# Where GpSimd applies the gains and biases of two inner norms, and which engine splits one weight piece

## The chip, the core and the metric

The kernel runs on one core of one Trainium2 chip. The metric is device time in microseconds (us): the median of 3 runs of the kernel before is 1522.11 us (1521.24 to 1522.42). A core has TensorE (PE in the profile, its weight loads PEld), VectorE (DVE), ScalarE (ACT), GpSimd (POOL) and SyncE (SP), which here only issues DMAs.

## What is computed

The reference is a two-layer decoder trunk on 256 tokens of width 1024. Layer 0 mixes tokens with a state-space layer and a GLU, then runs a dense SwiGLU. Layer 1 mixes with a three-group dilated attention and runs a top-2-of-8 expert SwiGLU. After each of these four sublayers comes the same residual and norm:

```
h = _s5_mixer(x, ...)
x = _layer_norm(DEEPNORM_ALPHA * x + h, ln_g[0, 0], ln_b[0, 0])     # norm 0
f = _swiglu(x, ...)
x = _layer_norm(DEEPNORM_ALPHA * x + f, ln_g[0, 1], ln_b[0, 1])     # norm 1
h = _dilated_attention(x, ...)
x = _layer_norm(DEEPNORM_ALPHA * x + h, ln_g[1, 0], ln_b[1, 0])     # norm 2
f = _moe(x, ...)
x = _layer_norm(DEEPNORM_ALPHA * x + f, ln_g[1, 1], ln_b[1, 1])     # norm 3
```

with `_layer_norm` = (x - mean) / sqrt(var + eps) * g + b. The change concerns norms 0 and 1, called the first and the second norm here.

## The kernel before, in words

**Tokens and norms.** The residual lies in SBUF as two tiles `x1[0]`, `x1[1]` of 128 tokens x 1024 (the program names them `xx`). At a norm, for each tile t: `residual_steps` (L749, L750) adds the sublayer's output and takes statistics on VectorE; `ln_power` (L755 to L757) finishes the statistics, and GpSimd takes one power (128x1, tile `lr_`); `ln_root` (L763 to L765) corrects it on VectorE; `ln_scale` (L772) subtracts the mean and multiplies by the root, in two halves of 512 columns. Then `flips` (L782) lets TensorE transpose the eight 128x128 blocks, and `turned` (L792 to L798) applies gain and bias on the transposed side: blocks 0 to 3 by ScalarE (L792), 4 to 7 by VectorE (L793), then ScalarE rounds to fp32r (L797) and VectorE takes the remainder (L798), so that `xT[0]` and `xT[1]` hold high and low part. The next matmuls read these. Their order over blocks is `korder` = 0, 4, 1, 5, ...

The residual itself stays without gain and bias until `ln_affine` (L775, L776) puts them on, since the next norm adds to it: on GpSimd, a multiplication and an addition of 128x1024 for each tile, with the gain and bias rows from the tile `gb` (both rows on every partition, 1 MB, loaded by GpSimd's queue).

**First norm.** For t = 0 and then 1 the loop at L871 to L885 does `flips`, `turned` and 48 matmuls into `ab` (the first two weight pieces of the SwiGLU, L885). While t = 0 is turned, VectorE interleaves what is left of the residual of t = 1 (`weave`). At t = 1, after `turned`, `ws.split` splits the next weight pieces. Behind the loop GpSimd's queue holds, in this order: `ln_affine` of both tiles, the load of the second norm's rows into `gb` (L890), and the bias tables of the attention: 64 DMAs `skew<-vecs` (L897) and 32 DMAs `raw<-skew` (L903, L907).

**Second norm.** The loop at L971 and after does the same with 24 matmuls into `pv` (values, L970) for each tile. After `turned` of t = 0 one weight piece is split with GpSimd as the subtracting engine; behind the loop stands `ln_affine` of both tiles, and then the pool of `gb` is closed; three raw tiles (`ring4`) are laid where it was.

**Weights.** `Stream` loads pieces of 1 MB (`raw` tiles) on SyncE's queue in a fixed order, `seq`, into whichever tile is free, oldest first. `split` turns a piece into a pair of fp32r tiles (L109 a copy on ScalarE, L110 a subtraction, on VectorE unless another engine is given). `get` gives back what the last call used, splits as far ahead as there are pairs, and hands out the next piece. Every matmul on split operands is done as three passes.

**Attention.** A loop over 8 head pairs `hp`: three query-key pieces (L1100, one for each dilation group, in the order 1, 2, 0 but 0, 1, 2 at hp = 0), then two value pieces (L970), with the steps of the pair before (scores, softmax, transposes, products with the values) interleaved. GpSimd does two copies a pair (L1016). Behind the attention come norm 2, the routing and the experts, whose weight pieces (`in_moe`) come through the same stream.

Of the kernel before, what the change touches and what calls it, by code (L numbers as in the profile page):

```python
# [20 lines left out]
D, S, G, P, C, H = 1024, 256, 64, 64, 16, 16  # L21
# [19 lines left out]
def gorder(hp):  # L41

    return (1, 2, 0) if hp else (0, 1, 2)
# [107 lines left out]
def trunk(ctx: ExitStack, tc: tile.TileContext, a, out, dbg=None):  # L151
    nc = tc.nc
    ctx.enter_context(tc.manual_schedule())
    V, A, T, Q = nc.vector, nc.scalar, nc.tensor, nc.gpsimd

    def dump(name, ap):
        if dbg and name in dbg:
            nc.gpsimd.dma_start(out=dbg[name], in_=ap)

    def pool(name, bufs=1, **k):  # L160
        return tc.tile_pool(name=name, bufs=bufs, reuse_waits="tile", **k)
# [9 lines left out]
    seq = []  # L171
# [4 lines left out]
    for i in range(3 * NFP):  # L176
        seq.append((a["ffn"][i], 2048, True))
    for hp in range(8):
        qk = [(a["qk"][3 * hp + g], 2048, True) for g in gorder(hp)]
        v = [(a["wv"][2 * hp + i], 1536, True) for i in range(2)]  # L180
        seq += v + qk if hp == 0 else qk + v
# [3 lines left out]
    def gain_bias(i):  # L185

        return bass.AP(a["ln"].tensor, i * 2 * D, [[0, 128], [1, 2 * D]])
# [39 lines left out]
    ws = Stream(nc, seq + moe_seq, raw, pairs)  # L227
# [27 lines left out]
    M_, A_, S_ = ALU.mult, ALU.add, ALU.subtract  # L255
# [419 lines left out]
    def passes(hl_s, hl_m):  # L675
        return ((hl_s[0], hl_m[0]), (hl_s[0], hl_m[1]), (hl_s[1], hl_m[0]))
# [42 lines left out]
    x1 = [xx[:, D * i:D * i + D] for i in range(2)]  # L719
# [5 lines left out]
    gb = gbs.enter_context(pool("gb", side="right")).tile([128, 2 * D], F32, name="gb")  # L725
# [21 lines left out]
    def residual_steps(t, n, src):  # L747
        xs = x1[t][:, n * 512:n * 512 + 512]
        return [lambda: V.scalar_tensor_tensor(out=xs, in0=xs, scalar=ALPHA, in1=src, op0=M_, op1=A_),  # L749
                lambda: V.bn_stats(out=lst[:, t, n, :], in_=xs)]  # L750
# [21 lines left out]
            V.tensor_scalar(out=xs, in0=xs, scalar1=lmv[:, t, 0:1], scalar2=lr_[:, t, 1:2], op0=S_, op1=M_)  # L772

    def ln_affine(t, eng, gb=gb):
        eng.tensor_tensor(out=x1[t], in0=x1[t], in1=gb[:, 0:D], op=M_)  # L775
        eng.tensor_tensor(out=x1[t], in0=x1[t], in1=gb[:, D:2 * D], op=A_)  # L776

    def flips(t, pp):

        tr = [pp.tile([128, 4, 128], F32, tag="tr", name="tr") for _ in range(2)]  # L780
        for k in range(8):
            T.transpose(tr[k // 4][:, k % 4, :], x1[t][:, k * 128:k * 128 + 128], ident)  # L782
        return tr

    def turned(i, t, tr, lnw=None, plain=None):

        cs = slice(t * 128, t * 128 + 128)
        f_ = lnw.tile([128, 8, 128], F32, tag="lnf", name="lnf") if plain is None else plain[:, :, cs]
        for j in range(5):
            if j < 4:  # L790
                g_, b_ = ([lnT[:, i, q, k:k + 1] for k in (j, 4 + j)] for q in range(2))
                A.activation(out=f_[:, j, :], in_=tr[0][:, j, :], func=ACTF.Identity, scale=g_[0], bias=b_[0])  # L792
                V.tensor_scalar(out=f_[:, 4 + j, :], in0=tr[1][:, j, :], scalar1=g_[1], scalar2=b_[1], op0=M_, op1=A_)  # L793
                yield
            if plain is None and j:
                ks = slice(j - 1, j + 4, 4)
                A.copy(out=xT[0][:, ks, cs], in_=f_[:, ks, :])  # L797
                V.tensor_tensor(out=xT[1][:, ks, cs], in0=f_[:, ks, :], in1=xT[0][:, ks, cs], op=S_)  # L798
                yield

    def weave(main, other):
        for _ in main:
            if other:
                (other.pop(0) or int)()
        for f in filter(None, other):
            f()

    def after(r):
        return [None, None, r[0], None, r[1], None, lambda: ln_power(1), lambda: ln_scale(1)]
# [48 lines left out]
    def gated_in(ab):  # L858
        sl = fw.tile([128, 2, 256], F32, tag="sl", name="sl")
        A.activation(out=sl, in_=ab[0], func=ACTF.Silu)  # L860
        V.tensor_tensor(out=sl, in0=sl, in1=ab[1], op=M_)
        return sl
# [21 lines left out]
                for ip, (s_, m_) in enumerate(passes([q[:, k, cs] for q in xT], [q[:, k, :] for q in w13[i]])):  # L884
                    T.matmul(ab[i][:, t, :], lhsT=s_, rhs=m_, start=(k == 0 and ip == 0), stop=(k == 7 and ip == 2))  # L885
    lns.close()
    for t in range(2):
        ln_affine(t, Q)
        dump(f"x1_{t}", x1[t])
    Q.dma_start(out=gb, in_=gain_bias(1))  # L890
    h0 = gated_in(ab)


# [4 lines left out]
    for i, b in enumerate(btab):  # L898
        hs = slice(4 * i, 4 * i + 4)
        for cl in range(2):  # L900
            pp = slice(64 * cl, 64 * cl + 64)
            for c0, b0, nb in ((0, 0, 4), (384, 4, 2)):
                Q.dma_start(out=b[pp, :, c0:c0 + 64 * nb],  # L903
                            in_=skew[:, hs, b0 + 1 - cl:b0 + nb + 1 - cl, :].rearrange("t h b s -> t h (b s)"))
            for g in range(2):
                c0 = 256 + 64 * (g ^ cl)
                Q.dma_start(out=b[pp, :, c0:c0 + 64], in_=skew[:, hs, 7 + g, :])  # L907

    accs = ExitStack()
    def down_proj(t, n, w, j):  # L910
# [6 lines left out]
    for fp in range(1, NFP):  # L917
        ab = []
        for i in range(2):
            w = [q.rearrange("p (k c) -> p k c", c=256) for q in ws.get()]  # L920
# [18 lines left out]
        if fp < NFP - 1:  # L939
            w = [q.rearrange("p (f c) -> p f c", c=1024) for q in ws.get()]  # L940
# [24 lines left out]
    w = [[q[:, 0:1536].rearrange("p (k c) -> p k c", c=384) for q in ws.get(1 - hf, hold=hf == 1)] for hf in range(2)]  # L965

    def values(t, kk, w):
        x_ = [q[:, kk, t * 128:t * 128 + 128] for q in xT]
        for ip, (s_, m_) in enumerate(passes(x_, [q[:, kk % 4, :] for q in w])):
            T.matmul(ov[t], lhsT=s_, rhs=m_, start=(kk == 0 and ip == 0), stop=(kk == 7 and ip == 2))  # L970

    for t in range(2):
        weave(turned(1, t, flips(t, ptn), lnw),
              [] if t else after(residual_steps(1, 1, acc[1][1])))
        ws.split(ws.cur + 9 * t, V if t else Q)
        for kk in korder:
            values(t, kk, w[kk // 4])
    trs.close()
    accs.close()
    for t in range(2):  # L980
        ln_affine(t, Q)
    for t in range(2):
        dump(f"x2_{t}", x1[t])
    gbs.close()
    xps.close()
    ring4 = ctx.enter_context(pool("ring4", side="right"))
# [6 lines left out]
    with ExitStack() as e:  # L993
# [96 lines left out]
        prev = iter(())  # L1090
        for hp in range(8):
            par = hp % 2
            for g in gorder(hp):
                w = [q.rearrange("p (k c) -> p k c", c=256) for q in ws.get()]
                o = pqk.tile([128, 2, 256], F32, tag="qk", name="qkp")
                for qk in range(2):
                    for k in range(8):
                        w_ = [q[:, k, qk * 128:qk * 128 + 128] for q in w]
                        for ip, (s_, m_) in enumerate(passes(w_, [q[:, k, :] for q in xT])):
                            T.matmul(o[:, qk, :], lhsT=s_, rhs=m_, start=(k == 0 and ip == 0), stop=(k == 7 and ip == 2))  # L1100
                        if k % 2 == 1:
                            next(prev, None)
                if g == 0:
                    undilated(o)
                else:
                    A.mul(out=qT[par][g], in_=o[:, 0, :], mul=0.125)
                    V.tensor_copy(out=kT[par][g], in_=o[:, 1, :])
            if hp:
                ov = [pv.tile([128, 512], F32, tag=f"v{t}", name=f"pv{t}")[:, 0:384] for t in range(2)]
                for hf in range(2):  # L1110
                    w = [q[:, 0:1536].rearrange("p (k c) -> p k c", c=384) for q in ws.get()]
                    for k in range(4):
                        for t in range(2):
                            values(t, 4 * hf + k, w)
                        next(prev, None)
            for _ in prev:
                pass
            if hp in (2, 4, 6):
                ws.add(bts[hp // 2 - 1:hp // 2])

            for t, f in ((0, A.copy), (1, V.tensor_copy)):
                v, lo_, hi_ = vt[par][t], slice(0, 64), slice(64, 128)
                f(out=v[lo_, 0:256], in_=ov[t][lo_, 0:256])
                f(out=v[hi_].rearrange("p (a b) -> p a b", b=128)[:, 0:3:2, :],
                  in_=ov[t][hi_, 0:256].rearrange("p (a b) -> p a b", b=128))
                f(out=v[hi_, 128:256], in_=ov[t][lo_, 256:384])
                f(out=v[lo_, 256:384], in_=ov[t][hi_, 256:384])
            prev = attn_steps(hp)
# [8 lines left out]
        for n in range(2):  # L1137
            w = [q.rearrange("p (k c) -> p k c", c=512) for q in ws.get()]
# [4 lines left out]
        w = [[q.rearrange("p (k c) -> p k c", c=512) for q in ws.get(9, hold=n == 1)] for n in range(2)]  # L1143
# [438 lines left out]
    with ExitStack() as e:  # L1582
# [11 lines left out]
        c = CAPS[E - 1]  # L1594
# [128 lines left out]
```

## Time and profile before

| what | value |
|---|---|
| median of 3 runs | 1522.11 us |
| the profiled execution's own time | 1521.36 us |
| its span, first to last instruction | 1519.6 us |
| busy: PE, PEld, DVE, ACT, POOL | 1435.5, 1043.3, 545.2, 384.4, 117.3 us |
| mean granted clock of TensorE | 0.978 of 2.4 GHz |

The profile's times count from the span's start. A busy PE is not a PE at its peak, since the ends of matmuls are modelled. The granted clock has two levels: 1.00 is 2.4 GHz, 0.50 is 1.2 GHz; a stretch with a mean between the two was partly at either.

### The profile page before, as it was taken

What the parts mean: (1) busy time and instruction counts of PE and PEld (TensorE: products, weight loads), DVE (VectorE), ACT (ScalarE), POOL (GpSimd) and SP (SyncE); (2) the same over time, 40 slices, a digit from 0 to 9 for tenths busy, and PEclk for the clock granted to TensorE, in tenths of its full rate; (3) what the DMA queues carried; (4) which work ended last, traced back from release to release, by engine and by line L of the source; (5) the groups of instructions that cost most, each with busy time, mean ns of one, the idle gap of its engine ahead of it and who ended that gap; (6) DMA issues with size and microseconds to landing.
All of it is one profiled execution on the core that took longest, in us unless ns stands there. A gap on an engine that the chain in (4) does not pass through costs nothing. (4 is left out here: it accounts for less than half of the span.)

```text
span 1519.6 us, 32295 instructions
## 1 busy us (share of the span) xinstructions
PE 1435.5 (94%) x14108; PEld 1043.3 (69%) x14108; DVE 545.2 (36%) x1021; ACT 384.4 (25%) x633; POOL 117.3 (8%) x156
## 2 busy tenths in 40 slices
PE   7769899998999999999999899999999999999996
PEld 6658799996999999865454466654566666666552
DVE  9998754447656666560020010010100100100103
ACT  6525444433555545420110000010100100100100
POOL 0110574004000000001000000000000000000001
PEclk9989899999999999989999999999999999999998
DMA  6008389553544454559999999999999999999995
GB/s 257 7 30 304 117 289 268 195 179 139 194 152 156 155 180 179 188 205 371 426 426 426 425 425 425 425 426 426 425 425 425 418 397 403 371 366 389 409 426 214
DMA packets 68412, 458.31 MB, mean 302 GB/s; under 512 B 9041, under 2 KB 9716, under 8 KB 15780
## 3 DMA queue, kind: packets, MB, share of 16 engines
q1 hardware_dynamic: 62752, 443.63, 72.7%
q0 software_dynamic: 4272, 9.92, 2.2%
q10 hardware_dynamic: 1236, 2.58, 0.5%
q8 instruction: 115, 1.88, 0.5%
q14 instruction: 37, 0.30, 0.1%
HBM read 454.97 MB, written 3.48 MB: 302 GB/s over the span
## 5 line engine op out<-in xcount | busy, mean ns | idle before, releaser
L1381 PE MATMUL a<-raw,xe 128*64 128x256 f32 (+1 forms) x7152 | 516.3, 328 | 9.0 <-DMA raw<-in_moe 8.3
L1381 PEld LDWEIGHTS a<-raw,xe 128*64 128x64 f32 (+1 forms) x7152 | 351.6, 124 | 163.4 <-issue 25.6
L1381 PE MATMUL y<-raw,h 128*32 128x256 f32 (+1 forms) x1792 | 255.7, 488 | 6.4 <-DMA raw<-in_moe 5.4
L1450 DVE TENSOR_TENSOR sl<-sl,a 128x256 f32<-128x256 f32 (+1 forms) x56 | 27.3, 488 | 564.8 <-PE a L1381 564.5
L110 DVE TENSOR_TENSOR sp<-raw,sp 128x2048 fp32r<-128x2048 f32 (+1 forms) x83 | 181.7, 2195 | 98.3 <-ACT sp L109 98.3
L1381 PEld LDWEIGHTS y<-raw,h 128*32 128x32 f32 (+1 forms) x1792 | 89.9, 123 | 150.8 <-issue 118.2
L109 ACT CAST sp<-raw 128x2048 fp32r<-128x2048 f32 (+1 forms) x85 | 154.3, 1823 | 69.8 <-PE ab L926 32.8
L1100 PE MATMUL qkp<-xT,sp 128*128 128x256 f32 x1152 | 153.1, 287 | 0.0
L1448 ACT ACTIVATE sl<-a 128x256 f32<-128x256 f32 (+1 forms) x56 | 24.5, 438 | 503.9 <-PE a L1381 503.8
L1100 PEld LDWEIGHTS qkp<-xT,sp 128*128 128x128 f32 x1152 | 141.9, 191 | 1.9
L926 PE MATMUL ab<-xT,sp 128*128 128x256 f32 x960 | 117.0, 283 | 0.0
L926 PEld LDWEIGHTS ab<-xT,sp 128*128 128x128 f32 x960 | 116.5, 192 | 0.7
L970 PE MATMUL pv<-sp,xT 128*128 128x384 f32 x384 | 73.8, 346 | 3.6 <-ACT xT L797 2.0
L970 PEld LDWEIGHTS pv<-sp,xT 128*128 128x128 f32 x384 | 67.5, 193 | 6.8 <-DVE xT L798 3.6
L757 POOL TENSOR_TENSOR lr__1387<-lr__1387,mhalf 128x1 f32<-128x1 f32 x8 | 4.5, 569 | 855.6 <-DVE lr__1387 L756 855.6
L1410 ACT COPY h<-ht 128x256 f32<-128x256 f32 (+1 forms) x56 | 23.8, 426 | 180.9 <-PE ht L1409 180.1
L914 PE MATMUL facc<-sp,hh 128*128 128x512 f32 x176 | 54.4, 390 | 0.0
L690 PE MATMUL glu<-sp,xT 128*128 128x512 f32 x144 | 36.4, 412 | 4.6 <-DVE sp L110 4.6
L1433 DVE SCALAR_TENSOR_TENSOR xx<-so,by_i,xx 128x512 f32<-128x512 f32 x28 | 19.7, 745 | 57.7 <-PE so L1432 57.7
L472 PE MATMUL pu<-x0T,raw 128*128 128x256 f32 x128 | 30.3, 400 | 8.3 <-DMA raw<-in_w_in 8.3
L626 PE MATMUL y<-p,cpad 128*32 128x127 f32 (+1 forms) x512 | 22.4, 331 | 16.0 <-DVE p L613 12.3
L914 PEld LDWEIGHTS facc<-sp,hh 128*128 128x128 f32 x176 | 32.4, 188 | 6.3
(271 smaller groups left out, 1181.1 us busy)
## 6 DMA issues: line engine op xcount, KB each, us to landing
raw<-in_moe SPq DMA_DIRECT2D x334, 1024.0 KB, 19.4
raw<-in_ffn SPq DMA_DIRECT2D x33, 1024.0 KB, 6.1
raw<-in_qk SPq DMA_DIRECT2D x24, 1024.0 KB, 4.8
raw<-in_wv SPq DMA_DIRECT2D x16, 768.0 KB, 4.3
raw<-in_w_glu SPq DMA_DIRECT2D x8, 1024.0 KB, 5.2
raw<-in_w_o SPq DMA_DIRECT2D x4, 1024.0 KB, 4.8
raw<-in_w_in SPq DMA_DIRECT2D x3, 1024.0 KB, 10.4
skew<-vecs POOLq DMA_DIRECT2D x64, 36.0 KB, 4.3
```

The source lines that it names most:

```text
L109: self.nc.scalar.copy(out=h_, in_=t_)
L110: (eng or self.nc.vector).tensor_tensor(out=l_, in0=t_, in1=h_, op=ALU.subtract)
L472: T.matmul(pu[:, mm].rearrange("p a b -> p (a b)"), lhsT=w[:, k, mm * 128:mm * 128 + 128], rhs=x0T[:, k, :], start=(k == 0 and mm == mms[0 ...
L690: T.matmul(o[t], lhsT=s_, rhs=m_, start=(kk == 0 and i == 0), stop=(kk == 7 and i == 2))
L914: T.matmul(acc[t][n], lhsT=s_, rhs=m_, start=(j == 0 and f == 0 and ip == 0), stop=(j == NFP - 1 and f == 1 and ip == 2))
L926: T.matmul(o[:, f, :], lhsT=s_, rhs=m_, start=(k == 0 and ip == 0), stop=(k == 7 and ip == 2))
L970: T.matmul(ov[t], lhsT=s_, rhs=m_, start=(kk == 0 and ip == 0), stop=(kk == 7 and ip == 2))
L1100: T.matmul(o[:, qk, :], lhsT=s_, rhs=m_, start=(k == 0 and ip == 0), stop=(k == 7 and ip == 2))
L1381: T.matmul(o[n * g:n * g + n, oc:oc + c], lhsT=lhsT, rhs=rhs[:, c * g:c * g + c], start=start, stop=stop, tile_position=(0, n * g), skip_g ...
L1410: A.copy(out=h_[:, 0:q], in_=p_[:, 0:q])
L1448: A.activation(out=sl[:, 0:c], in_=ob[n, 0][:, 0:c], func=ACTF.Silu)
L1450: V.tensor_tensor(out=sl[:, 0:c], in0=sl[:, 0:c], in1=ob[n, 1][:, 0:c], op=M_)
```

## The change

1. The gain and bias rows of the second norm become a piece of the weight stream, unsplit, ahead of the pieces of head pair 3; the load into `gb` at L890 goes.
2. `ln_affine` works in two column halves of 512, each multiplied and then added to: four instructions a tile in place of two.
3. The `ln_affine` of the first norm stands behind the issue of the bias tables on GpSimd's queue.
4. At the second norm VectorE, not GpSimd, subtracts for the piece that is split after t = 0.
5. The `ln_affine` of the second norm stands at the start of head pair 3 of the attention, with the rows from the stream's tile.

```
@@ seq
     for hp in range(8):
+        if hp == 3:
+            seq.append((lambda: gain_bias(1), 2048, False))
         qk = [(a["qk"][3 * hp + g], 2048, True) for g in gorder(hp)]
@@ ln_affine
-        eng.tensor_tensor(out=x1[t], in0=x1[t], in1=gb[:, 0:D], op=M_)
-        eng.tensor_tensor(out=x1[t], in0=x1[t], in1=gb[:, D:2 * D], op=A_)
+        for c in (slice(0, 512), slice(512, 1024)):
+            for f in range(2):
+                eng.tensor_tensor(out=x1[t][:, c], in0=x1[t][:, c], in1=gb[:, f * D:f * D + D][:, c], op=A_ if f else M_)
@@ behind the first norm
     lns.close()
-    for t in range(2):
-        ln_affine(t, Q)
-        dump(f"x1_{t}", x1[t])
-    Q.dma_start(out=gb, in_=gain_bias(1))
     h0 = gated_in(ab)
@@ behind the bias tables
                 Q.dma_start(out=b[pp, :, c0:c0 + 64], in_=skew[:, hs, 7 + g, :])
+    for t in range(2):
+        ln_affine(t, Q)
+        dump(f"x1_{t}", x1[t])
@@ second norm
-        ws.split(ws.cur + 9 * t, V if t else Q)
+        ws.split(ws.cur + 9 * t)
         for kk in korder:
             values(t, kk, w[kk // 4])
     trs.close()
     accs.close()
-    for t in range(2):
-        ln_affine(t, Q)
-    for t in range(2):
-        dump(f"x2_{t}", x1[t])
     gbs.close()
@@ attention
             par = hp % 2
+            if hp == 3:
+                w = ws.get()
+                for t in range(2):
+                    ln_affine(t, Q, w)
+                    dump(f"x2_{t}", x1[t])
             for g in gorder(hp):
```

## Rows read from the trace of the kernel before

**Rows 1.** Windows (SwiGLU, attention, experts): bounds, length, busy (count) by engine, PEclk, DMA share, GB/s.

```profile
183.00:336.00 153.00, 153.00 (x1086) 144.46 (x1085) 79.37 (x50) 64.41 (x49) 49.72 (x89) 1.00 0.74 238
383.00:636.00 253.00, 253.00 (x2064) 237.43 (x2063) 154.47 (x277) 131.76 (x217) 6.35 (x16) 1.00 0.48 172
...
1010.00:1040.00 30.00, 30.00 (x226) 16.07 (x224) 1.66 (x5) 2.54 (x7) 0.00 (x0) 1.00 1.01 426
```

**Rows 2.** Windows of the two tiles of the first and of the second norm.

```profile
158.79:167.09 8.30, 7.30 (x57) 6.68 (x56) 6.64 (x15) 3.53 (x9) 2.00 (x2) 1.00 0.00 1
167.09:183.37 16.28, 10.35 (x58) 9.66 (x59) 12.78 (x15) 7.34 (x11) 12.39 (x12) 0.69 0.20 79
358.89:365.88 6.99, 6.00 (x33) 4.78 (x31) 5.51 (x17) 4.86 (x9) 0.66 (x1) 1.00 0.01 2
365.88:381.76 15.88, 9.03 (x35) 6.96 (x35) 13.68 (x10) 3.51 (x9) 14.43 (x5) 0.79 0.34 133
```

**Rows 3.** Timeline of PE, first norm: start, length, engine, line, operation, count, [idle before].

```profile
171.05 1.97 PE L782 MATMUL tr<-idn,xx 128*128 128x128 f32 x8 [3.96 <-DVE xx L772]
```

**Rows 4.** Timeline of DVE, first norm.

```profile
157.51 0.22 DVE L763 SCALAR_TENSOR_TENSOR lr__1387<-lr__1387 128x1 f32<-128x1 f32 x1 [0.75 <-POOL lr__1387 L757]
...
165.67 2.32 DVE L763 SCALAR_TENSOR_TENSOR lr__1387<-lr__1387 128x1 f32<-128x1 f32 x1 [0.67 <-POOL lr__1387 L757]
...
168.22 2.19 DVE L765 TENSOR_TENSOR lr__1387<-lr__1387 128x1 f32<-128x1 f32 x1
170.45 1.00 DVE L772 TENSOR_SCALAR xx<-xx,lmv,lr__1387 128x512 f32<-128x512 f32 x2
...
179.08 0.43 DVE L798 TENSOR_TENSOR xT<-lnf,xT 128x256 fp32r<-128x256 f32 x1 [0.20 <-ACT xT L797]
```

**Rows 5.** Timeline of POOL, first norm.

```profile
165.61 2.38 POOL L775 TENSOR_TENSOR xx<-xx,gb 128x1024 f32<-128x1024 f32 x1
...
178.86 3.77 POOL L897 DMA_DIRECT2D skew<-vecs  x7
```

**Rows 6.** Timeline of DVE, second norm.

```profile
359.96 0.73 DVE L793 TENSOR_SCALAR lnf<-tr,lnT 128x128 f32<-128x128 f32 x2 [0.69 <-PE tr L782]
...
365.55 5.19 DVE L772 TENSOR_SCALAR xx<-xx,lmv,lr__1387 128x512 f32<-128x512 f32 x2
```

**Rows 7.** Timeline of POOL, second norm.

```profile
365.88 4.57 POOL L110 TENSOR_TENSOR sp<-raw,sp 128x2048 fp32r<-128x2048 f32 x1 [1.01 <-ACT sp L109]
```

**Rows 8.** Groups of POOL by line and shape: names, shapes, count | busy us, mean ns | idle.

```profile
L1566 POOL TENSOR_TENSOR raw<-raw,raw 128x512 f32<-128x512 f32 x1 | 1.3, 1263 | 0.0
```

**Rows 9.** Timelines of head pairs 2 and 3: POOL, DVE, PE, SP.

```profile
454.62 0.85 POOL L1016 CAST qq<-qq 64x256 fp32r<-64x256 f32 x2 [31.67 <-ACT qq L1009]
...
457.70 2.29 DVE L110 TENSOR_TENSOR sp<-raw,sp 128x2048 fp32r<-128x2048 f32 x1 [0.20 <-ACT sp L109]
...
463.93 0.87 PE L1100 MATMUL qkp<-xT,sp 128*128 128x256 f32 x6
...
411.93 15.88 SPq L74 DMA_DIRECT2D raw<-in_qk  x3
```

**Rows 10.** Timeline of PE, second norm.

```profile
360.92 4.96 PE L970 MATMUL pv<-sp,xT 128*128 128x384 f32 x24 [0.99 <-ACT xT L797]
...
372.67 2.93 PE L970 MATMUL pv<-sp,xT 128*128 128x384 f32 x8 [1.00 <-ACT xT L797]
```

**Rows 11.** Timeline of PE, two waits in the state-space layer.

```profile
90.11 0.64 PE L626 MATMUL y<-p,cpad 128*32 128x128 f32 x16 [2.47 <-DVE p L613]
...
99.22 0.64 PE L626 MATMUL y<-p,cpad 128*32 128x128 f32 x16 [2.40 <-DVE p L613]
```

**Rows 12.** Windows behind these two waits, columns as in the first group.

```profile
90.11:96.50 6.39, 5.76 (x83) 4.95 (x84) 6.29 (x13) 2.23 (x4) 1.28 (x1) 0.73 0.01 3
99.22:103.00 3.78, 2.76 (x65) 1.75 (x65) 3.68 (x9) 0.33 (x2) 1.28 (x1) 1.00 0.00 0
```

## The prediction
> **What bounds the kernel now.** I read the windows first. Through the SwiGLU and the attention TensorE is busy 153.00 of 153.00 and 253.00 of 253.00 us at full clock [rows 1]: nothing that VectorE, GpSimd or a queue does there shows in the time as long as it keeps ahead of TensorE. In the experts the DMA share is 1.01 at 426 GB/s [rows 1], so there weight loads set the pace. The change touches two more places, the norms before and after the SwiGLU, and there the same view gives the clue. Each norm handles two token tiles with equal work on TensorE: 8 transposes, then 48 matmuls (first norm) or 24 (second). Yet the first tile takes 8.30 and 6.99 us, the second 16.28 and 15.88, with a mean granted clock of 0.69 and 0.79 [rows 2].
>
> The timelines tell why. In the first norm TensorE waits 3.96 us for VectorE's scaled residual, L772 [rows 3]. VectorE is late since two tiny instructions of 128x1, L763 and L765, took 2.32 and 2.19 us, where L763 took 0.22 for the first tile [rows 4]. The first ends at 167.99, when GpSimd's multiplication does (165.61 + 2.38) [rows 4, 5]: an instruction of VectorE that reads two SBUF operands stands still while GpSimd's runs. In the second norm the two halves of L772 take 5.19 us [rows 6] where 1.00 was enough [rows 4]; GpSimd's subtraction for a weight piece (4.57 us) lies across them [rows 7].
>
> **The change, part by part.**
>
> First norm: GpSimd's four long instructions leave the second tile. Without the blocks L763 and L765 lose 2.32 - 0.22 = 2.10 and about 2.19 - 0.22 = 1.97, so L772 starts at 170.45 - 4.07 = 166.4 [rows 4], before TensorE is through with the first tile (167.09). The remainders, L798, are not blocked either. So the second tile should take what the first did: 16.28 - 8.30 = **7.98 us off** [rows 2]. The least would be the wait alone, 3.96 [rows 3], if the clock fell all the same. I take 7.98: the first tile is the same work without GpSimd. Late next would be the split of the next SwiGLU piece, queued behind `turned` on ScalarE and VectorE. It moves forward with the remainders; one subtraction, 2.29 us [rows 9], bounds what may show, and I take 0, since the first tile kept step although VectorE did the other tile's residual between.
>
> GpSimd's queue: the 64 + 32 DMA issues of the bias tables follow the second power at once, at 165.6 rather than 178.86 [rows 5], and lose the load of `gb` ahead of them. They now lie beside the second tile. An issue takes 3.77 / 7 = 0.54 us, and beside such issues L798 took 0.43 [rows 4, 5]. No row has L772 beside issues, so its cost lies between 0 and 2 x 0.54 = 1.1 us (each half waits for one issue); a gain is excluded, since an issue does no work of VectorE's. I take 0, by L798, the nearest row. The Trainium skill speaks against this (SBUF — State Buffer, "Who interferes with whom"): a VectorE instruction in a mode that takes both port pairs and GpSimd contend, and the one that comes second is fully blocked; it says the same of descriptor writing. By that rule the sum would be up to 1.1 us smaller, by the row it is not; no run here shows which.
>
> Gains and biases of the first norm go behind the tables, so they run in the SwiGLU. They become 8 instructions of 1.263 us [rows 8], 10.1 us. VectorE is busy 79.37 of 153 us there [rows 1], and a blocked instruction waits for one of GpSimd's, 1.26 us at most. What hides that is the lead of the splits over TensorE. Cost 0; without that cover up to 10.1 us. The residual that needs them comes only at the second norm.
>
> Second norm: VectorE's L772 for the second tile starts at 365.55 as now [rows 6] and ends 1.00 later [rows 4], at 366.55. Then VectorE does the split itself: 2.29 us [rows 9], to 368.84. Queued behind it is L793, and for that ScalarE's rounding and TensorE wait. From L793 to the first matmul it took 360.92 - 359.96 = 0.96 us for the first tile [rows 6, 10]; so matmuls start at 369.80 and with 4.96 us [rows 10] end at 374.76 instead of 381.76 [rows 2]: **7.00 us off** at full clock. GpSimd's gains and biases no longer block L798 here.
>
> The clock may take some back. TensorE would stand idle from about 367.2 (half of L772 at 366.55, then four transposes) to 369.8, some 2.6 us. Behind a wait of 2.47 us the clock fell, behind one of 2.40 it held [rows 11, 12]. After the 2.47 us the mean was 0.73 over 6.39 us, so it was at 1.2 GHz for 6.39 x 0.27 / 0.5 = 3.5 us [rows 12]; in the second norm now for 15.88 x 0.21 / 0.5 = 6.7 us [rows 2]. At the lower level one of these matmuls takes 2.93 / 8 = 0.366 us, at the higher 4.96 / 24 = 0.207 [rows 10], so 3.5 us at the lower level cost 3.5 / 0.366 x 0.159 = 1.5 us, and 6.7 us cost 2.9. Ends 0 and 2.9; I take **1.5 us back**, by the wait of 2.47, which is nearest.
>
> The piece with the rows: 1 MB on SyncE's queue replaces 1 MB on GpSimd's; the DMA share is 0.48 in the attention [rows 1]. Loads run far ahead: the first of pair 3, by count of the pieces, is issued at 411.93, and TensorE begins that pair at 463.93 [rows 9], so the rows, just ahead of it in the queue, have landed long before. GpSimd comes to its eight instructions right behind its copies of pair 2, at 455.5 [rows 9], and needs 10.1 us and what VectorE holds it up. VectorE's split at 457.70 may wait 1.26 us; it ended at 459.99, and the pair it feeds begins at 463.93 [rows 9]: a slack of 3.9 us takes that. The load into the tile that the rows leave waits on SyncE for GpSimd's last instruction, and all later loads behind it; the pieces loaded ahead cover that. Cost 0, bound 0 to 1.3 us, one block on the path. The tiles of `ring4` no longer wait for GpSimd, so their loads only come earlier. Four more instructions on GpSimd in each place cost its fixed part alone, 2 x 1.263 - 2.38 = 0.15 us a pair [rows 5, 8].
>
> All work behind the second norm starts earlier by the sum, the experts' loads too, since their buffers come free with the attention's progress.
>
> Sum: 7.98 + 7.00 - 1.5 = 13.5 us. Against the profiled execution's 1521.36 that is 1507.9; the median of the runs lies 0.75 higher, at 1522.11, so 1508.6.
>
> **The rivals.**
> - The clock holds at the second norm: 15.0 off, 1507.1. For it speaks the wait of 2.40, against it that of 2.47.
> - Low clock for 6.7 us: 12.1 off, 1510.0; with the late split (2.3) and one block in the attention (1.3) 8.5 off, 1513.6.
> - DMA issues block L772 in the first norm: 12.4 off, 1509.7. For it: L772 was blocked by GpSimd in rows 6; against it: L798 beside issues. The Trainium skill's rule named above would have it so.
> - In the first norm only the wait goes, since the clock falls there all the same: 3.96 + 5.5 = 9.5 off, 1512.6. Against it: it held through the first tile [rows 2].
> - The experts swallow it: loads are their bound [rows 1], and if the stream could not start earlier the end would stay, 1522.1. Against it: it starts in buffers that the attention frees.
> - Slower: in the two new places VectorE's waits reach TensorE one for one. All 16 instructions come to 16 x 1.263 = 20.2 us [rows 8], against 13.5 gained: 6.7 slower, 1528.8. It decides once two thirds get through, which asks that the splits have no lead; the 3.9 us of slack speak against it.
>
> **How the numbers follow.** Forecast 0.47; clock holds 0.23; low clock for longer 0.12; issues 0.07; only the wait 0.05; swallowed 0.03; slower 0.03. The range goes from 1505.5 (clock holds, and 1.6 for the spread of the runs, 1.2, and what is rounded above) to 1513.5, by the second rival with all its bounds; that leaves out some 0.08. 0.2%, or 3.0 us, is about what a measurement of this kernel can tell from no change; the first five cases lie beyond it: faster 0.94, same 0.03, slower 0.03.
>
> **What would show it.** Right: in both second tiles L763 and L765 at 0.2 us, L798 at 0.4 and L772 at 1.0 for two; second tiles of about 8.3 us and 8.9 to 10.5; no wait of 3 us before L782; TensorE without idle time in the SwiGLU and the attention; GpSimd's eight short instructions twice, in the SwiGLU and behind the copies of pair 2. Wrong: TensorE waiting for L110 in those windows, L772 far over 1.0, or the experts' first matmuls earlier and the end where it was.

## The result, and the profile after

The changed kernel takes 1506.32 us (median of 4 runs, 1505.60 to 1509.61) against 1522.26 for the kernel before (4 runs): a ratio of 0.9895, 95% interval [0.9878, 0.9912]. That is 15.9 us less, inside the stated range of 1505.5 to 1513.5 and 2.3 below the forecast of 1508.6. The profiled execution took 1505.60 us, with a span of 1503.8 where it was 1519.6: 15.8 us less.

The windows of the two tiles of both norms, the SwiGLU, the attention and the routing, in the changed kernel; columns as in [rows 1]:

```profile
158.78:166.91 8.13, 7.14 (x57) 6.70 (x57) 6.36 (x19) 3.54 (x9) 1.84 (x3) 1.00 0.01 2
166.91:175.07 8.16, 7.16 (x58) 6.73 (x57) 5.62 (x11) 7.10 (x11) 8.16 (x17) 1.00 0.28 71
350.75:357.76 7.01, 6.01 (x33) 4.79 (x31) 5.53 (x17) 4.85 (x9) 0.66 (x1) 1.00 0.01 2
357.76:367.31 9.55, 6.95 (x32) 6.67 (x33) 5.65 (x11) 3.25 (x9) 0.00 (x0) 0.82 0.59 220
175.00:348.00 173.00, 173.00 (x1218) 162.96 (x1218) 91.07 (x60) 70.12 (x54) 64.94 (x89) 1.00 0.69 227
369.00:622.00 253.00, 253.00 (x2064) 237.36 (x2063) 156.65 (x277) 131.63 (x216) 22.68 (x24) 1.00 0.49 175
...
642.51:674.23 31.72, 28.99 (x206) 20.56 (x204) 18.00 (x70) 7.54 (x17) 1.13 (x2) 0.84 0.63 253
```

These answer to [rows 2] and [rows 1]. The first norm's second tile now takes what the first takes, 8.16 after 8.13 us, at full clock. The second norm's takes 9.55 where it took 15.88, with a mean clock of 0.82: it still has a wait and a low stretch. TensorE is busy through the SwiGLU and the attention as before, although GpSimd now works there (22.68 us in the attention's window instead of 6.35).

TensorE's timeline at both norms shows the same, with the routing behind the attention for the ledger:

```profile
166.91 1.09 PE L785 MATMUL tr<-idn,xx 128*128 128x128 f32 x8
169.00 6.23 PE L888 MATMUL ab<-sp,xT 128*128 128x256 f32 x48 [1.00 <-ACT xT L800]
175.07 5.93 PE L928 MATMUL ab<-xT,sp 128*128 128x256 f32 x48
...
352.78 4.98 PE L972 MATMUL pv<-sp,xT 128*128 128x384 f32 x24 [0.99 <-ACT xT L800]
358.01 1.11 PE L785 MATMUL tr<-idn,xx 128*128 128x128 f32 x8 [0.25 <-DVE xx L774]
361.48 6.00 PE L972 MATMUL pv<-sp,xT 128*128 128x384 f32 x24 [2.35 <-ACT xT L800]
...
642.51 1.03 PE L785 MATMUL tr<-idn,xx 128*128 128x128 f32 x8
...
674.23 0.44 PE L1412 MATMUL ht<-idn,sl 128*128 128x128 f32 x2
```

And VectorE's, with GpSimd's DMA issues in the first line; these answer to [rows 4] and [rows 6] (L763, L772, L793, L798 are L765, L774, L796, L801 now):

```profile
165.57 14.01 POOL L896 DMA_DIRECT2D skew<-vecs  x26
165.66 0.22 DVE L765 SCALAR_TENSOR_TENSOR lr__1387<-lr__1387 128x1 f32<-128x1 f32 x1 [0.67 <-POOL lr__1387 L759]
...
166.10 0.16 DVE L767 TENSOR_TENSOR lr__1387<-lr__1387 128x1 f32<-128x1 f32 x1
166.29 1.00 DVE L774 TENSOR_SCALAR xx<-xx,lmv,lr__1387 128x512 f32<-128x512 f32 x2
...
357.40 1.00 DVE L774 TENSOR_SCALAR xx<-xx,lmv,lr__1387 128x512 f32<-128x512 f32 x2
358.32 2.29 DVE L110 TENSOR_TENSOR sp<-raw,sp 128x2048 fp32r<-128x2048 f32 x1
360.52 0.73 DVE L796 TENSOR_SCALAR lnf<-tr,lnT 128x128 f32<-128x128 f32 x2
```

In the two norms no instruction of VectorE stands still any more. At the second norm the order on VectorE is plain: scaling, subtraction for the weight piece, and only then L796, for which TensorE waits 2.35 us.

**Where the time went.** TensorE began the SwiGLU's next pieces at 183.21 before and at 175.07 now: 8.1 us. The attention's first matmuls (L1100, now L1103) moved from 381.61 to 367.31, 14.3: another 6.2. Through the attention nothing was added: norm 2's first transposes moved from 656.81 to 642.51, again 14.3. From there to the first transposes of the experts it took 32.98 us at a mean clock of 0.79 before, 31.72 at 0.84 now: 1.3. The experts gave 0.2. Sum 8.1 + 6.2 + 1.3 + 0.2 = 15.8.

Of the kernel before, TensorE behind the two norms and the same routing window:

```profile
183.21 5.92 PE L926 MATMUL ab<-xT,sp 128*128 128x256 f32 x48
...
381.61 18.15 PE L1100 MATMUL qkp<-xT,sp 128*128 128x256 f32 x150
...
656.81:689.79 32.98, 30.48 (x206) 21.66 (x204) 18.10 (x70) 7.55 (x17) 1.12 (x2) 0.79 0.63 253
```

### The profile page after: what moved, and what is told of

It is laid out like the page before. It is cut to its first block, busy times and chain, and to the rows that moved or that the text cites. A ratio compares the mean times of both kernels' runs of the same rounds, so it can differ in the third digit from the quotient of the medians.

```text
span 1503.8 us, 32304 instructions
## 1 busy us (share of the span) xinstructions
PE 1431.1 (95%) x14108; PEld 1040.5 (69%) x14108; DVE 534.7 (36%) x1022; ACT 384.0 (26%) x633; POOL 125.9 (8%) x162
## 5 line engine op out<-in xcount | busy, mean ns | idle before, releaser
L110 DVE TENSOR_TENSOR sp<-raw,sp 128x2048 fp32r<-128x2048 f32 (+1 forms) x84 | 187.9, 2243 | 98.3 <-ACT sp L109 98.3
L1103 PE MATMUL qkp<-xT,sp 128*128 128x256 f32 x1152 | 153.1, 287 | 0.0
L1103 PEld LDWEIGHTS qkp<-xT,sp 128*128 128x128 f32 x1152 | 141.9, 191 | 1.9
L692 PEld LDWEIGHTS glu<-sp,xT 128*128 128x128 f32 x144 | 28.7, 201 | 11.7 <-DVE sp L110 5.1
```

The lines of the kernel that those rows point to most:

```text
L110: (eng or self.nc.vector).tensor_tensor(out=l_, in0=t_, in1=h_, op=ALU.subtract)
L692: T.matmul(o[t], lhsT=s_, rhs=m_, start=(kk == 0 and i == 0), stop=(kk == 7 and i == 2))
```

## The experiments

### The parts alone

`e1_first_only` is the kernel before with one move:

```
     lns.close()
-    for t in range(2):
-        ln_affine(t, Q)
-        dump(f"x1_{t}", x1[t])
-    Q.dma_start(out=gb, in_=gain_bias(1))
     h0 = gated_in(ab)
...
                 Q.dma_start(out=b[pp, :, c0:c0 + 64], in_=skew[:, hs, 7 + g, :])
+    for t in range(2):
+        ln_affine(t, Q)
+        dump(f"x1_{t}", x1[t])
+    Q.dma_start(out=gb, in_=gain_bias(1))
```

> The kernel before, with the gains and biases of the first norm alone (and the load of the second norm's rows) moved behind the bias tables. Theory (GpSimd's instructions in the first norm's second tile stalled VectorE, and nothing else moved): the second tile of the first norm takes 8.2 us instead of 16.3, TensorE begins the SwiGLU's second pair of pieces near 175.1, the second norm keeps its second tile of 15 to 16 us, and the whole is 8 us faster (ratio 0.9947), give or take 1.5 us for where the low clock falls later. Rival (the DMA issues that now lie beside the tile block VectorE): the tile takes 9.3 us or more.

Measured: 1513.48 us, ratio 0.9942 [0.9923, 0.9961]. TensorE's timeline behind the two norms:

```profile
175.16 5.93 PE L926 MATMUL ab<-xT,sp 128*128 128x256 f32 x48
...
374.12 16.12 PE L1100 MATMUL qkp<-xT,sp 128*128 128x256 f32 x133
```

The first norm's second tile takes 8.2 us (167.00 to 175.16), and that of the second norm still 16.2 (357.9 to 374.12). The theory holds, and the rival's 9.3 us beside the DMA issues did not come. The whole is 9 us faster rather than 8: 7.5 are there at the attention's first matmul (374.12 for 381.61), and the other 1.5 lie in the experts, whose length varies between profiles by more than that (see the last point of the next section).

`e2_second_only` is the changed kernel with `ln_affine` of the first norm back between the norm and the bias tables:

```
     lns.close()
+    for t in range(2):
+        ln_affine(t, Q)
+        dump(f"x1_{t}", x1[t])
     h0 = gated_in(ab)
...
-    for t in range(2):
-        ln_affine(t, Q)
-        dump(f"x1_{t}", x1[t])
 
     accs = ExitStack()
```

> The changed kernel, with the gains and biases of the first norm put back between the first norm and the bias tables. Theory (the two places add up): the first norm's second tile takes 16.3 us again, the second norm's second tile 9 to 10, and the whole stands 6 to 7.5 us under the kernel before, ratio 0.9950 to 0.9960. Rival (the second norm's gain needs the first's, or the extra came from the weight stream): under 4 or over 9 us.

Measured: 1513.43 us, 0.9934 [0.9915, 0.9952], 9.2 us less than before. That misses the 6 to 7.5 us expected and lies at the rival's mark of 9, so the total alone would speak for the rival. The trace does not. VectorE and TensorE at the first norm:

```profile
165.75 1.24 DVE L765 SCALAR_TENSOR_TENSOR lr__1387<-lr__1387 128x1 f32<-128x1 f32 x1 [0.67 <-POOL lr__1387 L759]
...
168.36 2.86 DVE L774 TENSOR_SCALAR xx<-xx,lmv,lr__1387 128x512 f32<-128x512 f32 x2
...
182.13 5.92 PE L928 MATMUL ab<-xT,sp 128*128 128x256 f32 x48
```

TensorE begins the SwiGLU's next pieces at 182.13, only 1.1 us earlier than before: L765 takes 1.24 us where it took 2.32 before (as L763), since GpSimd's instructions are now half as long, but the halves of L774 are stopped too. The second norm's second tile takes 7.9 us (365.07 to 372.93), less than the 9 to 10 expected. Its timeline, and its window (columns as in [rows 1]):

```profile
365.07 1.11 PE L785 MATMUL tr<-idn,xx 128*128 128x128 f32 x8 [0.24 <-DVE xx L774]
368.54 4.55 PE L972 MATMUL pv<-sp,xT 128*128 128x384 f32 x24 [2.36 <-ACT xT L800]
372.93 1.35 PE L1103 MATMUL qkp<-xT,sp 128*128 128x256 f32 x10
...
365.07:372.93 7.86, 5.50 (x33) 5.06 (x33) 5.41 (x10) 3.25 (x9) 0.00 (x0) 1.00 0.49 194
```

TensorE waits 2.36 us as in the changed kernel, but the clock did not fall (1.00 through the tile), so the 24 matmuls took 4.55 where they took 6.00 there. The second norm alone is worth more when the clock holds, and the halves help the first norm a little: 8.7 us are there at the attention's first matmul (372.93 for 381.61), and the rival is not needed.

### Which engine subtracts at the second norm

`e3_gpsimd_split` is the changed kernel with that part undone:

```
-        ws.split(ws.cur + 9 * t)
+        ws.split(ws.cur + 9 * t, V if t else Q)
```

> The changed kernel, with GpSimd again subtracting for the piece that is split after the second norm's first tile. Theory (a GpSimd instruction with two SBUF inputs stalls VectorE's second half of the scaling for its whole 4.6 us): that half ends 4 us late, TensorE waits about 4 us for the transposes, the clock falls, the second norm's second tile takes 12.5 to 14.5 us instead of 9.3, and the whole is 3 to 5 us slower than the changed kernel. Rival (the split's place does not matter, the gains and biases alone did the harm): within 1 us of the changed kernel.

Measured: 1510.54 us, 0.9917 [0.9898, 0.9935], 4.2 us above the changed kernel. Its timeline of TensorE has the old wait again:

```profile
362.73 1.12 PE L785 MATMUL tr<-idn,xx 128*128 128x128 f32 x4 [3.98 <-DVE xx L774]
364.85 7.25 PE L972 MATMUL pv<-sp,xT 128*128 128x384 f32 x24 [1.00 <-ACT xT L800]
371.93 18.15 PE L1103 MATMUL qkp<-xT,sp 128*128 128x256 f32 x150
```

VectorE's two halves took 5.19 us, as in [rows 6]; the second tile ends 4.6 us later than in the changed kernel (371.93 for 367.31).

`e8_vector_split_only` does that part alone, in the kernel before:

```
-        ws.split(ws.cur + 9 * t, V if t else Q)
+        ws.split(ws.cur + 9 * t)
```

> The kernel before, with VectorE subtracting for the piece at the second norm and nothing moved. Theory (GpSimd's next work takes the place of the split): GpSimd comes to the gains and biases 4.6 us earlier, right behind its second power, and stalls L763, L765 and VectorE's split there as in the first norm; the second tile stays at 14 to 18 us and the whole within 2 us of before. Rival (the split alone was the harm): L772 takes 1.0 us for both halves at 365.6 and the tile shrinks by 3 us or more.

Measured: 1521.21 us, 0.9993 [0.9983, 1.0002]: nothing. The timelines of GpSimd and VectorE there show the pattern of the first norm, at the second:

```profile
364.02 2.37 POOL L775 TENSOR_TENSOR xx<-xx,gb 128x1024 f32<-128x1024 f32 x1
...
364.09 2.31 DVE L763 SCALAR_TENSOR_TENSOR lr__1387<-lr__1387 128x1 f32<-128x1 f32 x1 [0.45 <-POOL lr__1387 L757]
...
366.63 2.20 DVE L765 TENSOR_TENSOR lr__1387<-lr__1387 128x1 f32<-128x1 f32 x1
368.86 1.00 DVE L772 TENSOR_SCALAR xx<-xx,lmv,lr__1387 128x512 f32<-128x512 f32 x2
```

GpSimd, freed of the subtraction, begins its multiplication at 364.02 and stalls L763 and L765 instead. So the split's move alone is worth nothing. The gains' move alone is worth something: e3, which has it, begins the attention at 371.93, and e1, which has neither of the two moves, at 374.12, 2.2 us later. The whole gain at this norm needs both.

### What in GpSimd's work stalls VectorE

`e7_memset` is the kernel before, with GpSimd's work at the first norm replaced; it leaves out the first norm's gains and biases:

```
     lns.close()
-    for t in range(2):
-        ln_affine(t, Q)
-        dump(f"x1_{t}", x1[t])
+    for i in range(6):
+        Q.memset(bts[i % 4], 0.0)
     Q.dma_start(out=gb, in_=gain_bias(1))
```

> The kernel before, with the first norm's gains and biases on GpSimd left out of the residual and six memsets of 128x2048 (about 1.8 us each, on tiles that the bias tables fill later) at their place. Theory (what stalls VectorE is GpSimd reading SBUF, while it reads two operands itself): memsets read nothing, so L763 and L765 stay at 0.2 us, the second tile takes 8.2 us, 8 us faster than before. Rival (any long GpSimd instruction stalls VectorE): L763 or L765 take 1 us or more and the tile stays over 12 us.

Measured: 1520.52 us, 0.9986 [0.9977, 0.9996]. The expectation was missed, and the timelines of VectorE, GpSimd and TensorE say why:

```profile
165.77 0.22 DVE L763 SCALAR_TENSOR_TENSOR lr__1387<-lr__1387 128x1 f32<-128x1 f32 x1 [0.67 <-POOL lr__1387 L757]
...
166.21 0.16 DVE L765 TENSOR_TENSOR lr__1387<-lr__1387 128x1 f32<-128x1 f32 x1
166.41 6.87 DVE L772 TENSOR_SCALAR xx<-xx,lmv,lr__1387 128x512 f32<-128x512 f32 x2
...
165.68 11.09 POOL L888 MEMSET raw<- 128x2048 f32 x6
...
171.31 1.12 PE L782 MATMUL tr<-idn,xx 128*128 128x128 f32 x4 [4.13 <-DVE xx L772]
```

L763 and L765 ran through beside the memsets, as the theory says. But L772 took 6.87 us for its halves, TensorE waited 4.13 us for it, and the tile took 16.1 us (167.00 to 183.08), as long as before. So there are two ways of standing still: an instruction with two SBUF operands waits for a GpSimd instruction that reads, one of L772's kind waits for one that only writes, too. The Trainium skill has both rules (SBUF — State Buffer, "Who interferes with whom"): two SBUF inputs contend with GpSimd's reads and not with its writes alone, and an instruction in a two-port mode, which `tensor_scalar` can enter, contends with GpSimd altogether. This trace agrees, with 0.22 and 6.87 us. The theory named only the first.

### How much cover the new places have

`e6_wide` undoes the halves in the changed kernel:

```
-        for c in (slice(0, 512), slice(512, 1024)):
+        for c in (slice(0, 1024),):
```

> The changed kernel, with GpSimd's instructions 1024 columns wide again (4 in place of 8 at each place). Theory (the width matters only for how long one block lasts, and there is cover): GpSimd's stretches stay at about 16 us, single blocks of VectorE grow to 2.4 us, TensorE waits for nothing, time within 1 us of the changed kernel. Rival (the halves are what keeps VectorE in time): TensorE waits in the SwiGLU or the attention and the time is 1 us or more longer.

Measured: 1506.18 us, 0.9886 [0.9870, 0.9903]: no difference to the changed kernel. GpSimd needs 13.7 us in the SwiGLU and 15.7 in the attention, and TensorE waits for nothing in either. Where they stand now, the halves do nothing that the time shows.

`e5_gpsimd_x3` adds two instructions behind each of GpSimd's:

```
                 eng.tensor_tensor(out=x1[t][:, c], in0=x1[t][:, c], in1=..., op=A_ if f else M_)
+                for o in (A_, S_):
+                    eng.tensor_tensor(out=x1[t][:, c], in0=x1[t][:, c], in1=gb[:, 0:D][:, c], op=o)
```

> The changed kernel, with GpSimd's work at both new places tripled: behind each multiplication and each addition the gain row is added and taken off again (24 instructions of 128x512 in place of 8; the residual changes by rounding alone). Theory (both places have cover): VectorE's splits there slow down for some 50 us each, TensorE still waits for nothing in the SwiGLU and the attention, and the time is within 1 us of the changed kernel. Rival (the cover was nearly used up): TensorE waits for VectorE's split there, up to 20 us in all, or SyncE's queue is held by the load behind GpSimd's last instruction until TensorE runs out of pieces.

Measured: 1516.61 us, 0.9953 [0.9937, 0.9970], 10.3 us above the changed kernel, so the expectation was missed. In the SwiGLU tripled work costs nothing. In the attention GpSimd is busy with it from 442.5 to 489.7, and TensorE stands, for a reason neither theory named. The timelines of TensorE and GpSimd:

```profile
361.56 7.18 PE L974 MATMUL pv<-sp,xT 128*128 128x384 f32 x24 [2.36 <-ACT xT L802]
...
490.15 0.58 PE L1029 MATMUL sc<-kk,qq 128*128 128x256 f32 x1 [5.85 <-POOL qq L1016]
490.66 0.58 PE L1031 MATMUL sc<-kk,ql 64*128 64x256 f32 x1
...
442.53 1.29 POOL L779 TENSOR_TENSOR xx<-xx,raw 128x512 f32<-128x512 f32 x1
...
484.96 4.68 POOL L781 TENSOR_TENSOR xx<-xx,raw 128x512 f32<-128x512 f32 x2
489.70 0.85 POOL L1016 CAST qq<-qq 64x256 fp32r<-64x256 f32 x2
```

Queued behind the extra instructions are GpSimd's copies of head pair 3, and the scores of that pair wait for them: 5.85 us, after which the clock was low for some 7 us (0.50 from 490 to 496, 0.68 from 496 to 498, then 1.00). The 7.18 above is 1.2 more than the changed kernel's 6.00, at the same wait. So VectorE's splits are not what gives first here; GpSimd's own queue is. In the changed kernel the copies come 15 us behind the last gain, which its timeline of GpSimd shows:

```profile
441.26 16.65 POOL L779 TENSOR_TENSOR xx<-xx,raw 128x512 f32<-128x512 f32 x8
472.92 0.85 POOL L1014 CAST qq<-qq 64x256 fp32r<-64x256 f32 x2 [15.01 <-ACT qq L1007]
```

### A version that beats both

What is left at the second norm is the 2.29 us of the split ahead of L796. `e4_late_subtract` keeps ScalarE's copy for that piece where it is and moves VectorE's subtraction, with the return of the raw tile, behind the turning of the second tile:

```
-        ws.split(ws.cur + 9 * t)
+        if t == 0:
+            assert ws.nsplit == ws.cur
+            half = ws.split_hi()
+        else:
+            ws.split_lo(*half)
+            ws.split(ws.cur + 9)
...
+    def split_hi(self):
+        i = self.nsplit
+        _, n, _ = self.seq[i]
+        t, pair = self.loaded.pop(i), self.pairs.pop(0)
+        self.nc.scalar.copy(out=pair[0][:, 0:n], in_=t[:, 0:n])
+        self.nsplit += 1
+        return i, n, t, pair
...
+    def split_lo(self, i, n, t, pair):
+        self.nc.vector.tensor_tensor(out=pair[1][:, 0:n], in0=t[:, 0:n], in1=pair[0][:, 0:n], op=ALU.subtract)
+        self.ready[i] = pair
+        self.back(t)
+        self.load()
```

> The changed kernel, with VectorE's subtraction for that piece put behind the turning of the second norm's second tile (ScalarE's copy stays). Theory (the subtraction of 2.29 us lies on the chain from the scaling to the first matmul): TensorE's wait behind the transposes falls from 2.35 to 1.0 us, the clock does not fall there, the second tile takes 7.0 us instead of 9.3, and the piece is ready near 364.3, before TensorE needs it near 364.9; the whole is 2.4 us faster than the changed kernel. Rival (the piece then comes late): TensorE waits up to 1 us for it and the gain is 1.5 us or less.

Measured: 1503.65 us, 0.9873 [0.9855, 0.9892]. TensorE's timeline, and the subtraction on VectorE's:

```profile
358.13 1.11 PE L799 MATMUL tr<-idn,xx 128*128 128x128 f32 x8 [0.26 <-DVE xx L788]
360.24 4.55 PE L986 MATMUL pv<-sp,xT 128*128 128x384 f32 x24 [0.99 <-ACT xT L814]
364.62 3.58 PE L1122 MATMUL qkp<-xT,sp 128*128 128x256 f32 x28
...
362.49 2.28 DVE L127 TENSOR_TENSOR sp<-raw,sp 128x2048 fp32r<-128x2048 f32 x1
```

The wait is 0.99, the clock holds (1.00 from 358.13 to 364.66), and the next piece's matmuls begin at 364.62 without a wait, with the subtraction done at 362.49 + 2.28 = 364.77: just in time, since the first two of the three passes need only ScalarE's half. Against the changed kernel's 367.31 this is 2.7 us. Both once more, side by side on one chip:

> The version with the late subtraction once more, beside the changed kernel on the same chip. Theory (the subtraction lay on the second norm's chain): 2 to 3 us under the changed kernel, second tile 7.0 us, no fall of the clock at the second norm. Rival (the difference seen before was the spread between chips and executions): within 1 us of the changed kernel.

> The changed kernel once more. Theory (8.1 us in the first norm, 7.0 less the cost of a low clock in the second, up to 1.5 either way from the low clock at the routing and the weight stream): 14 to 16.5 us under the kernel before; the second norm's second tile 8.0 to 10.5 us, depending on whether and how long the clock is low there. Rival (the 15.9 us seen before were luck of the executions): under 13 us.

Measured: 1503.24 us, 0.9879 [0.9863, 0.9896], for the late subtraction and 1506.35, 0.9905 [0.9888, 0.9921], for the changed kernel. The second pair differs by 3.1 us, a little more than the 2 to 3 expected; the first, whose two kernels ran apart, by 2.7. The four runs of each do not overlap in either pair (at most 1504.5 against at least 1505.5). The changed kernel stands 15.2 us under the kernel before here, within the 14 to 16.5 expected and above the rival's 13. The second norm looked the same in both profiles: 24 matmuls in 4.54 us with a wait of 1.00, and in 5.95 with a wait of 2.35.

## Why the prediction was right, point by point

**First norm, 7.98 us.** Measured 8.1. The second tile does equal the first (8.16 and 8.13), L763 and L765 take 0.22 and 0.16, and neither the fall of the clock nor a late split came. e1 shows it alone. The bound of 0 to 1.1 us for DMA issues beside L772 came out at 0: L774 took 1.00 for both halves at 166.29, with 26 issues in 14.01 us (0.54 each) from 165.57 on. The rule of the Trainium skill that spoke against the change (SBUF — State Buffer, "Who interferes with whom") was not met with here, though L772 was stopped by other GpSimd work. The reading behind the term was half of the cause: it named two SBUF operands, which fits L763 and L765, but not L772, which e7 shows is stopped even by work that only writes.

**Second norm, 7.00 less 1.5.** Measured 6.2. The chain came as written: halves of L772 in 1.00, the split in 2.29, L796 behind it, first matmul 0.96 later. From the start of the scaling to the first matmul it took 361.48 - 357.40 = 4.08 us, where the sum had 4.25. The mis-sized term is the 24 matmuls at full clock. The sum took 4.96 us from the first tile, but the second tile's take 4.55 (e2, e4): they wait 0.2 us in all for the remainders (L801), the first tile's 0.7. The low stretch had the size that was summed: 9.55 x 0.18 / 0.5 = 3.4 us at 1.2 GHz where the sum had 3.5, and 6.00 - 4.55 = 1.45 us lost where it had 1.5.

That this size came true is luck, for its reason failed. The wait was 2.35 us and not 2.6, so it was shorter than the 2.40 behind which the clock held in [rows 11, 12], and by the prediction's own comparison the clock should have held. In e2 it did hold, behind 2.36; in e5, behind 2.36 as well, the 24 matmuls took 7.18, 2.6 us more than at full clock and near the bound of 2.9. So the size of the wait does not tell, and what decides is shown by no run here. e3 and e8 show that the two parts need each other: the split alone is worth nothing without the gains' move, and the move alone leaves 4.2 us of the gain undone.

**SwiGLU and attention, 0.** Right: TensorE waits for nothing there. The rows' way through the weight stream was not tried by itself. GpSimd's eight instructions took 16.65 us in the attention instead of 10.1 at the least, since VectorE's splits hold them up and are held up (2.65 and 3.06 us for 2.29); e5 and e6 show that the cover is far from used up in the SwiGLU. One reading of the queue was short: I named VectorE's splits and SyncE's queue as what stands behind GpSimd's work in the attention. What gives first is GpSimd's own next copies, with 15 us to spare.

**Everything behind moves forward.** Right, so the rival by which the experts' loads would swallow the gain is out: 14.3 us at the second norm's end are 14.3 at norm 2 and 15.8 at the end. The rival of a slower kernel had both its places tried, at three times its work, and it stayed faster than before.

**What the sum lacked.** Of the 2.3 us between 13.5 and 15.8, the first norm gave 0.2, the second 0.7 (0.4 of it the matmuls, 0.2 the chain before them), the experts 0.2 and the routing 1.3. At the routing the clock was at 1.2 GHz for 32.98 x 0.21 / 0.5 = 13.9 us before and 31.72 x 0.16 / 0.5 = 10.2 us after. That is not the change's doing. Over the twelve profiles on record the same reckoning gives 13.9 us three times (the kernel before, e1 and e5) and 10.1 to 10.3 nine times, e7 and e8 among them, which are no faster than the kernel before. The experts vary as well, from 828.3 to 831.9 us. So 14.3 of the 15.8 us are shown to come from the change, and the other 1.5 lie in stretches that vary as much without it. It is luck, too, that the total of 1506.3 lies nearer to 1507.1, the rival in which the clock holds, than to the forecast of 1508.6: the clock did fall.

## What to carry to other kernels

Where two tiles with equal work take unequal time, look for what another engine does beside the slower one: here tiny VectorE instructions of ten times their length pointed to GpSimd. Work that feeds only a much later step goes to a stretch where TensorE is the bound, but look at what follows in the same queue: in e8 the next instruction of GpSimd took the place of the one that was moved, and nothing was gained. And count what stands behind moved work on its own engine's queue first.

## What the runs showed of the hardware that was not expected

- GpSimd's memsets, which read nothing, left VectorE's two-operand instructions alone (0.22 and 0.16 us) and stopped the halves of L772 (6.87 us for 1.00).
- The stall goes both ways: in the attention one of GpSimd's instructions of 128x512 took 3.35 us where 1.29 was the median, beside a subtraction of VectorE's.
- The same wait of TensorE, 2.35 to 2.36 us before the second norm's second matmuls, left the clock up in one kernel (e2) and brought it down in others; the 24 matmuls behind it took 4.55 us there, 6.00 in the changed kernel and 7.18 in e5.
